# A two-layer hybrid trunk on eight cores: casts of layer 1 into the first FFN phase, residual loads put off, more staging, first loads first

## The chip, the cores and the metric

The kernel runs on the 8 cores of one Trainium2 chip, one batch element per core, with no exchange between the cores. The time is the device time of the slowest core in microseconds (us).

Executions come in two states. In the fast one all cores show a mean granted TensorE clock of 0.973 to 0.989 of full speed. In the slow one the four cores of a die, sometimes of both dies, show a lower one: in one run cores 0 to 3 had a clock of 0.893 to 0.895, while cores 4 to 7 had 0.988. Only fast runs, or the cores of the undisturbed die, are compared here.

## The reference, cut to what matters

```python
D_MODEL, BATCH, SEQ, DEPTH = 1024, 8, 8192, 2
def reference(x, ...):
    h = x
    for l in range(DEPTH):
        mix = token_mixer(h, ...)     # q, k, v, gates; sliding window + forgetting attention; projections
        h = layer_norm(DEEPNORM_ALPHA * h + mix, ...)      # residual 1
        ffn = conv_gated_ffn(h, ...)  # D_FF 2816, 3 causal taps, silu gate
        h = layer_norm(DEEPNORM_ALPHA * h + ffn, ...)      # residual 2
    return h
```

All inputs are float32. The kernel multiplies in bf16, so every weight is cast once on its way.

## The kernel before

The kernel works in four phases: mixer 0, FFN 0, mixer 1, FFN 1, each over 16 tiles of 512 tokens. PE is TensorE, DVE VectorE, ACT ScalarE, POOL GpSimd, SP SyncE. Two engines issue DMAs. POOL issues those that cast float32 to bf16; SP issues the rest, all in one program order:

```python
def cast_some(n=1):                    # POOL: weights float32 in HBM -> bf16 copy in HBM
    for _ in range(n):
        if casts:                      # 30 of layer 0 (w_f1, w_f2), then 76 of layer 1
            key, dst, src = casts.pop()
            i = len(casts) % 8
            POOL.wait(cast_last[i])
            cast_tok[key] = cast_last[i] = POOL.dma(dst, src, so(f"wcast{i}"))
...
# main loop of the mixer: t is the time that the program's builder reckons for PE
if l == 0 and dn.step > 3 and POOL.t <= t and t >= cast_t:
    cast_some()
    cast_t = t + 20e3                  # one every 20 us, all of them in mixer 0
```

The residual of the next tile is loaded into `hf`, the same buffer from which the norm's result has just been stored. The load is therefore behind a wait for that store:

```python
# Norm.apply: the second half of the tile leaves for H1T, then on_done follows at once
SP.wait(t_o)
hf_free[0] = SP.dma(self.hdst_v[:, m - 3:m + 1, ts(self.T)], hf[:, m - 3:m + 1, :], so("hout"))
if m == KC - 1:
    ...
    self.on_done(hf_free[0])           # load_hf(T + 1)
...
def load_hf(self, T):
    SP.wait(hf_free[0], src_tok(self.hsrc, T))      # all later SP work waits here too
    hf_tok[0] = SP.dma(hf, self.hsrc_v[:, :, ts(T)], so("hin"))
```

Q and K go through a ring of staging buffers to HBM, and the attention loads them back in chunks, with V (`kch`, `vch`):

```python
self.st = Ring([E(f"st{i}", [TT], BF16) for i in range(4)])
...
si, sbuf, sfree = st.get()
DVE.wait(sfree)                        # the store of four evictions ago must have landed
t_ev = DVE.sig(nc.vector.tensor_scalar(out=sbuf, in0=bank, ...))
SP.wait(t_ev)
SP.dma(dst[2 * c, 0:64, tsl], sbuf[0:64, :], ...)
```

At the start the constants come first: six loads on SP, memsets, a wait of all engines for them, 32 small stores on SP; after that wait, from POOL, the first activations (`hbp`) and eight weight chunks (`wring`). In layer 0 each chunk is loaded with a cast by POOL and its bf16 copy is stored to `WMD` by SP. Before its first eviction DVE waits for a bias (`bvt`) and a mask.

The softmax here doesn't subtract the row's maximum and nothing guards it: scores larger than these inputs give would overflow.

## Time and profile before

| | us |
|---|---|
| fast runs, same rounds as the changed kernel | 10881, 10885 |
| profiled execution, slowest core (5) | 10831.6 |
| median core of that execution | 10786 |
| slow runs, left out | 11102, 11518 |

Five marks cut the span: the 4th and the 16th load of `hbg` (the gate's activations, one per tile) in each mixer, and the first one of mixer 1. Median over the eight cores of the profiled execution:

| stretch | before, us |
|---|---|
| start to 4th hbg load | 625 |
| mixer 0, 4th to 16th hbg load | 2649 |
| to the first hbg load of mixer 1 (FFN 0 lies here) | 2228 |
| mixer 1, first to 4th hbg load | 542 |
| mixer 1, 4th to 16th hbg load | 2474 |
| rest (FFN 1 lies here) | 2248 |

Mixer 0 and mixer 1 do the same work from the 4th to the 16th load. The prediction reads core 5, on which they are 2700 and 2484 us.

### The profile page before, as it was taken

The page shows a single profiled execution, that of the slowest core. Times are in us where ns is not written, and L with a number is a line of the kernel's source. Part 1 is how long each engine was busy: PE and PEld are TensorE (multiplying, and loading weights), DVE is VectorE, ACT ScalarE, POOL GpSimd, SP SyncE. Part 2 cuts the span into 40 slices and gives each one's busy share as a digit, 9 for nine tenths or more (in the row PEclk, how much of TensorE's full clock was granted, in tenths as well). Part 3 has the DMA queues.
Part 4 walks back from the last instruction along what each step waited for, and adds up shares of the span by engine and source line. Part 5 has one row for each costly group of instructions (what it writes and reads, how often), then busy time and mean ns, then how long its engine had stood idle before and what let it go on. Part 6 is the DMA issues. An engine that isn't in the chain of part 4 may idle for free.

```text
span 10831.6 us, 223078 instructions; the slowest of 8 cores (10746.5 to 10831.6 us)
## 1 busy us (share of the span) xinstructions
PE 10016.4 (92%) x77548; PEld 5139.1 (47%) x77548; DVE 4816.6 (44%) x7633; ACT 6399.9 (59%) x12159; POOL 2722.5 (25%) x2510
## 2 busy tenths in 40 slices
PE   5998898998788999999989999999999889999998
PEld 2444454555455444444434455555555544444443
DVE  3544333332211465566555544333332226566655
ACT  2466787898788332333224678889999863233322
POOL 0212112111111344444431221111110214444444
PEclk8999999999899999999989999999999999999999
DMA  6766766666644311111136665555554441111111
GB/s 136 186 164 169 167 154 160 155 156 149 136 127 113 119 51 44 40 47 47 43 101 157 165 162 152 145 159 148 143 146 128 133 132 51 43 40 50 48 40 43
DMA packets 707722, 1231.95 MB, mean 114 GB/s; under 512 B 64016, under 2 KB 277392, under 8 KB 704400
## 3 DMA queue, kind: packets, MB, share of 16 engines
q1 hardware_dynamic: 595920, 1055.02, 33.3%
q0 software_dynamic: 110720, 162.64, 11.0%
q8 instruction: 662, 10.85, 0.4%
q14 instruction: 420, 3.44, 0.1%
HBM read 1181.07 MB, written 246.69 MB: 132 GB/s over the span
## 4 chain that ended last, share of the span: by engine, by line
PE 66%; POOL 7%; DVE 7%; ACT 7%; DMA 7%; issue 5%; SPq 1%; another core or an unknown queue 1%; DVEq 0%; POOLq 0%; ACTq 0%
PE pD L536 15%; PE pA L877 9%; PE pO L916 7%; PE pB L536 6%; PE pB L877 5%; POOL hf L374 3%; PE pA L1224 3%; PE pO L1224 3%; PE pD L1224 3%; PE pB L1224 3%; ACT pr_134 L886 2%; ACT pr_240 L886 2%; POOL hf L376 2%; SPq L101 1%; PE pA L1186 1%
## 5 line engine op out<-in xcount | busy, mean ns | idle before, releaser
L886 ACT ACTIVATE pr_134<-pA 128x512 bf16<-128x512 f32 (+2 forms) x2414 | 1467.6, 638 | 346.6 <-PE pA L877 280.2
L886 ACT ACTIVATE pr_240<-pA 128x512 bf16<-128x512 f32 (+2 forms) x2414 | 1467.2, 638 | 215.5 <-PE pA L877 149.9
L886 ACT ACTIVATE pr_134<-pB 128x512 bf16<-128x512 f32 (+2 forms) x1330 | 885.3, 666 | 164.9 <-PE pB L877 136.5
L886 ACT ACTIVATE pr_240<-pB 128x512 bf16<-128x512 f32 (+2 forms) x1330 | 885.6, 666 | 103.4 <-PE pB L877 76.8
L374 POOL TENSOR_TENSOR hf<-hf,mean 128x512 f32<-128x512 f32 x512 | 716.8, 1400 | 377.9 <-DVE hf L370 360.9
L326 ACT ACTIVATE sq_60<-hf 128x512 f32<-128x512 f32 x256 | 161.4, 630 | 621.6 <-DVE hf L1227 494.9
L326 ACT ACTIVATE sq_61<-hf 128x512 f32<-128x512 f32 x256 | 161.4, 630 | 615.7 <-DVE hf L1227 525.2
L336 POOL TENSOR_TENSOR acc_q<-acc_q,sq_61 128x512 f32<-128x512 f32 x256 | 324.9, 1269 | 684.3 <-ACT sq_61 L326 680.7
L101 POOL DMA_DIRECT2D hbg_163<-xT x16 | 14.6, 915 | 1563.8 <-PE pO L916 960.3
L370 DVE TENSOR_TENSOR hf<-hf,rstd 128x512 f32<-128x512 f32 x512 | 405.3, 807 | 1.0 <-DVE mean L365 0.5
L101 POOL DMA_DIRECT2D hbg_269<-H2T x16 | 14.2, 886 | 1524.4 <-PE pO L916 1332.6
L916 PEld LDWEIGHTS pO<-vch_0_127,pr_134 128*128 128x128 bf16 x4640 | 269.7, 98 | 204.5 <-issue 27.3
L336 POOL TENSOR_TENSOR acc_q<-acc_q,sq_60 128x512 f32<-128x512 f32 x192 | 243.3, 1267 | 486.5 <-ACT sq_60 L326 483.9
L916 PEld LDWEIGHTS pO<-vch_0_129,pr_134 128*128 128x128 bf16 x4640 | 270.8, 99 | 198.9 <-issue 25.7
L916 PEld LDWEIGHTS pO<-vch_1_233,pr_240 128*128 128x128 bf16 x4640 | 267.9, 98 | 193.7 <-issue 14.8
L916 PEld LDWEIGHTS pO<-vch_1_235,pr_240 128*128 128x128 bf16 x4640 | 267.5, 98 | 191.0 <-issue 13.2
L334 DVE TENSOR_TENSOR acc_r<-acc_r,hf 128x512 f32<-128x512 f32 x448 | 318.0, 710 | 49.8 <-DVE hf L1227 3.2
L916 PEld LDWEIGHTS pO<-vch_0_128,pr_134 128*128 128x128 bf16 x4160 | 240.0, 98 | 180.1 <-issue 20.5
L916 PE MATMUL pO<-vch_0_127,pr_134 128*128 128x65 bf16 x4640 | 315.0, 195 | 10.6 <-issue 10.6
L916 PEld LDWEIGHTS pO<-vch_1_234,pr_240 128*128 128x128 bf16 x4160 | 239.6, 98 | 174.9 <-issue 14.6
L916 PE MATMUL pO<-vch_0_129,pr_134 128*128 128x65 bf16 x4640 | 315.8, 195 | 1.1 <-issue 1.1
L916 PE MATMUL pO<-vch_1_233,pr_240 128*128 128x65 bf16 x4640 | 312.8, 194 | 0.0
(1969 smaller groups left out, 24749.5 us busy)
## 6 DMA issues: line engine op xcount, KB each, us to landing
H1T<-hf SPq DMA_DIRECT2D x64, 1024.0 KB, 5.5
hf<-H1T SPq DMA_DIRECT2D x32, 2048.0 KB, 9.2
hf<-xT SPq DMA_DIRECT2D x16, 2048.0 KB, 12.5
H2T<-hf SPq DMA_DIRECT2D x32, 1024.0 KB, 4.4
hf<-H2T SPq DMA_DIRECT2D x16, 2048.0 KB, 11.4
outT<-hf SPq DMA_DIRECT2D x32, 1024.0 KB, 4.0
wring_1_260<-WMD SPq DMA_DIRECT2D x90, 256.0 KB, 3.6
wring_1_261<-WMD SPq DMA_DIRECT2D x90, 256.0 KB, 3.8
```

The source lines that it names most:

```text
L101: self.e.dma_start(out=out, in_=in_, **kw).then_inc(so.sem, 16)
L326: t_q = ACT.sig(nc.scalar.activation(out=sqb, in_=hf[:, m, :], func=AF.Square))
L334: self.r = DVE.sig(nc.vector.tensor_tensor(out=acc_r, in0=acc_r, in1=hf[:, m, :], op=ALU.add))
L336: self.q = POOL.sig(nc.gpsimd.tensor_tensor(out=acc_q, in0=acc_q, in1=sqb, op=ALU.add))
L370: t = DVE.sig(nc.vector.tensor_tensor(out=hf[:, i, :], in0=hf[:, i, :], in1=rstd, op=ALU.mult))
L374: t_p = POOL.sig(nc.gpsimd.tensor_tensor(out=hf[:, m, :], in0=hf[:, m, :], in1=mean_s, op=ALU.add))
L376: t_o = POOL.sig(nc.gpsimd.tensor_scalar(out=hf[:, m, :], in0=hf[:, m, :], scalar1=self.g_t[:, m:m + 1], scalar2=self.b_t[:, m:m + 1], op0 ...
L536: ins = mm(out, lhsT=lhs(i), rhs=rhs(i), start=(i == 0), stop=(i == n - 1))
L877: ins = mm(sbank[:, c0:c0 + w], lhsT=K[:, jl * 128:(jl + 1) * 128], rhs=Q[:, q0:q0 + w], start=fresh, stop=not diag, skip_group_check=diag)
L886: t_p = ACT.sig(nc.scalar.activation(out=pbuf[:, 0:tot], in_=sbank[:, 0:tot], func=AF.Exp, scale=0.125))
L916: ins = mm(obank[:, i * 65:(i + 1) * 65], lhsT=pbuf[:, cc:cc + 128], rhs=V[:, j % CKB, :], start=state["first"], stop=fin, skip_group_chec ...
L1224: ins = mm(bank, lhsT=wo[m][:, f, :], rhs=at[:, f, :], start=(f == 0), stop=(f == FC - 1))
```

## The change

The intent is to take transfers out of the busy first mixer and put them where the DMA engines are less busy (18% in FFN 0), to keep SP from being held, and to start sooner. There are four parts. The four edits together give the changed kernel.

```diff
 # 1 casts
-            if casts:
-                key, dst, src = casts.pop()
+            if l in casts and casts[l]:
+                key, dst, src = casts[l].pop(0)
...
-                    cast_some()
-                    cast_t = t + 20e3
+                    cast_some(0)
+                    cast_t = t + 60e3
... in the FFN, after each f:
                     ln_step()
+                    if f % 4 == 3:
+                        cast_some(l + 1)
 # 2 residual loads put off: mixer, FFN
-  (lambda t_: self.load_hf(T + 1))
+  (lambda t_: lnq.append((lambda: self.load_hf(T + 1), lambda: ready(t_) + 15e3)))
-  (lambda t_, T=T: self.load_hf(T + 1))
+  (lambda t_, T=T: lnq.extend([(lambda: None, None)] * 4 + [(lambda: self.load_hf(T + 1), None)]))
 # 3 staging
-  self.st = Ring([E(f"st{i}", [TT], BF16) for i in range(4)])
+  self.st = Ring([E(f"st{i}", [TT], BF16) for i in range(8)])
   ... (ons, onr move to another region for space)
 # 4 start
     stages[0].prefetch([])
+    constants()          # the block that stood ahead of everything, unchanged inside
...
-            DVE.wait(t_mk, t_bv)
+  (t_bv before its first use in proj, t_mk before its first use in swa)
```

More of the change, by code (lines that the diff above doesn't have):

```diff
@@ L252, in cvs @@
         return cv[l][:, a:a + n]
-    so_c = so("cst")
-    for l in range(DEPTH):
-        SP.dma(cv[l], cvec[l], so_c)
-        SP.dma(bfn[l], b_f[l], so_c)
-        t0 = SP.dma(esk[l], sinks[l].rearrange("(o n) -> o n", o=1).partition_broadcast(128), so_c)
-    so_p = so("cstp")
-    POOL.dma(identb, c_ident, so_p)
-    t1 = POOL.dma(negmb, c_negm, so_p)
-    ACT.wait(t0)
-    for l in range(DEPTH):
-        t_e = ACT.sig(nc.scalar.activation(out=esk[l], in_=esk[l], func=AF.Exp))
-    DVE.wait(t0, t1, t_e)
@@ L266, in build_program @@
-    nc.vector.memset(onesf, 1.0)
-    nc.vector.memset(eps1, EPS)
-    nc.vector.memset(eps4, 4.0 * EPS)
-    for l in range(DEPTH):
-        nc.vector.tensor_scalar(out=bfn[l], in0=bfn[l], scalar1=-1.0, scalar2=None, op0=ALU.mult)
-        nc.vector.tensor_scalar(out=cvs(l, "bg"), in0=cvs(l, "bg"), scalar1=0.5, scalar2=None, op0=ALU.mult)
-    ones8 = hf.rearrange("p a b -> p (a b)")[0:8, 0:768].bitcast(BF16).rearrange("p (a b) -> p a b", a=3)
-    eights = hf.rearrange("p a b -> p (a b)")[0:8, 1024:1792].bitcast(BF16).rearrange("p (a b) -> p a b", a=3)
@@ L274, in build_program @@
-    nc.vector.memset(ones8, 1.0)
-    t_c = DVE.sig(nc.vector.memset(eights, 8.0))
-    for E in ENGS:
-        E.wait(t_c)
-    for T in range(NT):
-        SP.dma(KBT[:, 64:67, ts(T)], ones8, so("cst8"))
-        t_c8 = SP.dma(QBT[:, 67:70, ts(T)], eights, so("cst8"))
     cast_tok = {}
-    casts = []
+    cast_last = [None] * 8
+    casts = {l: [] for l in range(DEPTH)}
     for l in range(DEPTH):
         if l > 0:
-            for c in range(NPROJ):
-                casts.append((("m", l, c), WMD[l, c], w_mix[l, c]))
-            casts.append((("v", l), WVD[l], w_v[l]))
-            for c in range(NPROJ, NCHUNK):
-                casts.append((("m", l, c), WMD[l, c], w_mix[l, c]))
-        for f in range(FC):
-            casts.append((("f1", l, f), WF1[l, f], w_f1[l, f]))
-        for m in range(KC):
-            casts.append((("f2", l, m), WF2[l, m], w_f2[l, m]))
@@ L296, in build_program, with cast_some @@
-    casts.reverse()
-    cast_last = [None] * 8
-    def cast_some(n=1):
+            casts[l] += [(("m", l, c), WMD[l, c], w_mix[l, c]) for c in range(NPROJ)]
+            casts[l] += [(("v", l), WVD[l], w_v[l])]
+            casts[l] += [(("m", l, c), WMD[l, c], w_mix[l, c]) for c in range(NPROJ, NCHUNK)]
+        casts[l] += [(("f1", l, f), WF1[l, f], w_f1[l, f]) for f in range(FC)]
+        casts[l] += [(("f2", l, m), WF2[l, m], w_f2[l, m]) for m in range(KC)]
+    def cast_some(l, n=1):
         for _ in range(n):
-            if casts:
-                key, dst, src = casts.pop()
-                i = len(casts) % 8
+            if l in casts and casts[l]:
+                key, dst, src = casts[l].pop(0)
+                i = len(cast_tok) % 8
@@ L310, in build_program @@
     hf_tok = [None]
-    hf_free = [t_c8]
+    hf_free = [None]
     lnq = []
@@ L385, in apply, with constants @@
                 self.a = t
+    def constants():
+        so_c = so("cst")
+        for l in range(DEPTH):
+            SP.dma(cv[l], cvec[l], so_c)
+            SP.dma(bfn[l], b_f[l], so_c)
+            t0 = SP.dma(esk[l], sinks[l].rearrange("(o n) -> o n", o=1).partition_broadcast(128), so_c)
+        so_p = so("cstp")
+        POOL.dma(identb, c_ident, so_p)
+        t1 = POOL.dma(negmb, c_negm, so_p)
+        ACT.wait(t0)
+        for l in range(DEPTH):
+            t_e = ACT.sig(nc.scalar.activation(out=esk[l], in_=esk[l], func=AF.Exp))
+        DVE.wait(t0, t1, t_e)
+        nc.vector.memset(onesf, 1.0)
+        nc.vector.memset(eps1, EPS)
+        nc.vector.memset(eps4, 4.0 * EPS)
+        for l in range(DEPTH):
+            nc.vector.tensor_scalar(out=bfn[l], in0=bfn[l], scalar1=-1.0, scalar2=None, op0=ALU.mult)
+            nc.vector.tensor_scalar(out=cvs(l, "bg"), in0=cvs(l, "bg"), scalar1=0.5, scalar2=None, op0=ALU.mult)
+        ones8 = hf.rearrange("p a b -> p (a b)")[0:8, 0:768].bitcast(BF16).rearrange("p (a b) -> p a b", a=3)
+        eights = hf.rearrange("p a b -> p (a b)")[0:8, 1024:1792].bitcast(BF16).rearrange("p (a b) -> p a b", a=3)
+        nc.vector.memset(ones8, 1.0)
+        t_c = DVE.sig(nc.vector.memset(eights, 8.0))
+        for E in ENGS:
+            E.wait(t_c)
+        for T in range(NT):
+            SP.dma(KBT[:, 64:67, ts(T)], ones8, so("cst8"))
+            t_c8 = SP.dma(QBT[:, 67:70, ts(T)], eights, so("cst8"))
+        hf_free[0] = t_c8
     def ln_step(n=1):
@@ L408, in __init__ @@
             self.sp = Ring([E(f"sp{i}", [TT], BF16) for i in range(4)])
-            self.ons = Ring([E(f"ons{i}", [4, 2, 64], BF16) for i in range(2)])
-            self.onr = Ring([E(f"onr{i}", [4, 128], BF16) for i in range(2)])
             E = Region(EA + 72 * 1024, EA + 88 * 1024, f"_{l}")
@@ L420, in __init__ @@
             self.sg = Ring([P(f"sg{i}", [TT], F32) for i in range(4)])
+            self.ons = Ring([P(f"ons{i}", [4, 2, 64], BF16) for i in range(2)])
+            self.onr = Ring([P(f"onr{i}", [4, 128], BF16) for i in range(2)])
             self.mk = P("mk", [2, 2, 512], BF16)
@@ L594, in proj @@
                 vi, svb, svfree = svr.get()
-                DVE.wait(svfree)
+                DVE.wait(svfree, t_bv)
                 vat = va[T % 2]
@@ L646, in swa @@
                 PE.wait(DVE.now())
+                DVE.wait(t_mk)
                 oat = oa[T % 3]
@@ L763, in post @@
                 nrm = Norm(db, eps4, cvs(l, "g1"), cvs(l, "b1"), self.hdst, self.hdst_v, T,
-                           (lambda t_: self.load_hf(T + 1)) if T + 1 < NT else (lambda t_: None))
+                           (lambda t_: lnq.append((lambda: self.load_hf(T + 1), lambda: ready(t_) + 15e3))) if T + 1 < NT else (lambda t_: None))
                 for m in range(KC):
@@ L1096, in run @@
             if l == 0:
-                cast_some(1000)
+                cast_some(0, 1000)
             if pre_next is not None:
@@ L1212, in run @@
                 elif pre_next is not None:
+                    cast_some(l + 1, 1000)
                     pre_next(now())
@@ L1216, in run @@
                 nrm = Norm(fb, eps1, cvs(l, "g2"), cvs(l, "b2"), self.hdst, self.hdst_v, T,
-                           (lambda t_, T=T: self.load_hf(T + 1)) if T + 1 < NT else (lambda t_: None))
+                           (lambda t_, T=T: lnq.extend([(lambda: None, None)] * 4 + [(lambda: self.load_hf(T + 1), None)])) if T + 1 < NT else (lambda t_: None))
                 for m in range(KC):
```

## The prediction

> **What bounds the kernel now.** Of the three timed runs of the kernel before, only the fastest, 10884.82 us, is near the profiled execution (10831.6 us on its slowest core, all cores within 0.8% of each other). The other two, 11102 and 11518 us, are the slow state and are left out, so I work from 10833 to 10885 us.
>
> I read the page's slices first. TensorE (PE) is busy 92% of the span, so the question is where the other 8% lies. The two FFN phases (third and fourth lines' right-hand clock digits all 9, DMA share 1) have almost no idle; the two mixers do, and the first mixer more than the second.
>
> ```profile
> PE   5998898998788999999989999999999889999998
> PEclk8999999999899999999989999999999999999999
> DMA  6766766666644311111136665555554441111111
> ```
>
> The two layers do the same work, so layer 1 is a control for layer 0. I took marks that both have (the loads of hbg, one per tile of 512 tokens, found in the timeline of POOL) and read the busy time between the same two marks of both layers. First column: the stretch, its length, then busy time and instruction count of PE, PEld, DVE, ACT, POOL, then clock, DMA share, GB/s.
>
> ```profile
> 619.00:3319.00 2700.00, 2414.59 (x24044) 1348.03 (x24045) 896.28 (x1645) 2122.95 (x3780) 409.21 (x416) 0.96 0.65 153
> 3627.00:5540.00 1913.00, 1861.53 (x8519) 834.30 (x8517) 1159.63 (x1509) 596.30 (x1601) 836.91 (x754) 1.00 0.18 51
> 6094.00:8578.00 2484.00, 2384.66 (x24031) 1336.09 (x24028) 892.76 (x1644) 2116.99 (x3779) 357.17 (x310) 0.99 0.56 147
> ```
>
> The same 24,000 matmuls took 2700 us in layer 0 and 2484 us in layer 1: 216 us more, of which 30 us are busy time at a lower granted clock (0.96 against 0.99) and 186 us are idle (285 against 99). What only layer 0 has there is the weight casts: 106 DMAs issued from POOL between 641 and 3175 us. The waits of PE and then of the SP queue in the layer 0 stretch show how they hurt:
>
> ```profile
> PE pA L877 <- DMA vch_0_129<-VBD: 50.8, 1, 50.8
> PE pD L607 <- DVE st_0_138 L573: 34.7, 3, 13.6
> PE pA L877 <- DMA vch_0_128<-VBD: 17.5, 1, 17.5
> PE pA L877 <- DMA vch_0_127<-VBD: 16.5, 1, 16.5
> ...
> SPq L86 <- DMA H1T<-hf: 192.6, 12, 57.2
> ```
>
> In layer 1 that last line reads 56.7 us, longest 7.0. SP issues K, V, weight and residual loads in one order; the residual load for the next tile (hf) must wait until the store of H1T has landed, and everything behind it waits too. In the worst case the store took 57 us beside a burst of eight casts that POOL let go at once after it had been held:
>
> ```profile
> 2828.31 3.94 POOL L101 DMA_DIRECT2D WF<-w_f  x8
> ```
>
> The start is the other piece. PE has its first weights at 36.3 us, does three groups, and then stands until 79.8 us:
>
> ```profile
> PE pD L536 <- DMA wring_0_154<-w_mix: 36.3, 1, 36.3
> ...
> PE pD L536 <- DVE qa_141 L566: 36.6, 1, 36.6
> ```
>
> The chain of waits through this window gives 23.36 us of that to the bias load bvt, which SP issued only at 55.39 us, behind 32 small constant stores and eight weight stores; DVE waited for it before its first eviction.
>
> **What the Trainium skill says.** The page "DMA: Bandwidth & Descriptors", section "Issuing engines are not separate DMA queues", says that DMAs of every issuing engine run on the same 16 DMA engines and interleave. The trace agrees: the casts are POOL's, yet SP's store of H1T took 57 us beside them, and a weight chunk landed in 4.0 to 4.5 us in layer 0 against 3.4 to 3.8 in layer 1. The same page, "SWDGE vs HWDGE vs iDMA", says a cast during DMA can only be issued from GpSimd, so the casts cannot leave POOL; only their time can change. "TensorE: Matmul & The Clock Gate", section "What's actually happening", says that the array falls to half clock after an idle window of about 3.4 us; this trace shows a granted clock of 0.50 in the 20 us stretches inside the 50.8 us stall and 0.83 just after it. A removed long stall is thus worth slightly more than its length.
>
> **The change part by part.** The order of instructions, with buffer numbers left out, is identical on PE, DVE and ACT. Only POOL (where casts stand) and SP (where 8 stores and the residual loads stand) differ, plus buffers and waits. So compute cost is unchanged and all of the effect is in waiting.
>
> 1. Casts. Layer 0's mixer keeps 30 of the 106 (22 w_f1 and 8 w_f2), placed singly or in twos, at most three, between POOL's other loads. 216 us over 106 casts is 2.04 us per cast, bursts included; 30 at that rate would cost 61 us. Alone, a cast moves about half or two thirds as much as an hbp load, and layer 1 has those without visible stalls, so I take about half the rate: 30 us. Gain 186 us, in which the 192.6 us of SP blocked on H1T is already contained.
>
> 2. The other 76 go to FFN 0, one per four f steps, five per tile, so all are out in the 16th tile. DMA is only 18% busy there. A cast issue takes POOL 0.5 us. In a tile's first ten f steps POOL is full: per step of 3.45 us it has a conv tap (1.2), two norm operations (1.26 and 1.01) and gaps. PE already loses 51 us over this phase to DVE line 1200, in 49 waits of 1 us, in just these steps. Two of the five casts fall there: 2 x 0.5 us x 16 = 16 us lost; the others fall in steps with 2.7 us of POOL idle and are free. The hb load comes behind a cast but has the second product, 8 x 4.75 = 38 us, to land (9.6 us alone). Cost 15 us.
>
> 3. Start. The first loads go out at about 2 us instead of 12.45, and without the 32 small stores beside them. Before, it took from 12.45 to 36.3 us to have the first weights. But the constants now stand behind eight stores on SP that each wait for a weight chunk, so they come at some 30 us, and PE's first group waits for them. I estimate PE's start at 40 to 50 us, and a wait at the ninth chunk, which POOL can issue only after its memsets. bvt is no longer in the way of the first eviction. The group that began at 79.8 us should begin around 50 and some of it is lost again: gain 25 us.
>
> 4. Staging of eight, residual loads 15 us later: in layer 1, without casts, PE waits some 20 us for staging buffers (8.5, 5.5, 3.3, 3.2) and a vch load (7.1). Most of it goes: 18 us there, and 10 in layer 0 beyond part 1. In the FFN the later residual load (at f = 13 or so of 22) leaves 30 us and the product for a load of 8 to 9 us: nothing either way.
>
> Sum: 186 - 15 + 25 + 28 = 224 us. From 10833 to 10885 this gives 10609 to 10661; I say **10640 us**, a ratio of 0.980 to the fast runs.
>
> **The rivals.** (a) The stall moves instead of going: SP stays held by the waits for POOL's norm before each H1T store (79 us in layer 0, 84 in layer 1) and for PE releases, and 30 casts of the larger kind still meet the K and V loads. For it: the casts kept are the big ones, 1.5 and 2.1 MB of traffic each against 0.75 for a w_mix chunk, so by bytes 36% stay though only 28% by count. Against it: layer 1 has the same SP waits and only 99 us idle. It would leave 80 us of the 216, a time near 10700. (b) POOL becomes the bound of FFN 0: every cast displaces a conv tap, and DVE and PE follow: 76 casts at 1 us, 60 us more than I count, also near 10700. Against it: 837 us of 1913 busy. (c) The casts were most of the trouble and the staging much of the rest, so layer 0 comes out equal to layer 1 and both mixers lose further waits: 216 + 35 + 40 - 10 = 281, near 10580. (d) The start does not shorten, as the constants on SP arrive later than I think: 25 us off, 10665.
>
> **Range and chances.** The gain lies between about 130 us, (a) and (b) partly together, and 320 us. On fast runs that is 10515 to 10755. Two of three runs before were slow by 2 and 6%, so a median with slow runs in it could lie higher; I set 10520 to 10860. The expected gain is almost exactly 2%, so the verdict is nearly even: faster 0.53, same 0.46, slower 0.01.
>
> **What would show each step.** Part 1: in the stretch between the same hbg marks of layer 0, span about 2510 to 2530 us (2700 before), PE idle near 120 us, SP's wait for H1T from 193 to below 40 us. Part 2: FFN 0 within 20 us of its 1913, waits on line 1200 up from 51 to about 65. Part 3: the fourth group of PE near 50 us, the wait on qa gone. Part 4: waits on st below 10 us in all. I am wrong if layer 0's stretch stays above 2600 us (then the casts were not the cause), if FFN 0 grows by over 40 us, or if the start is no earlier.

## More of the kernel before

Where such an undisturbed part is used, the cores and their clock are named.

The median of each stretch is taken by itself, so the column does not sum to the median span.

## The result

The changed kernel's fast runs took 10587.38 and 10605.22 us, and those of the kernel before in the same rounds 10881.27 and 10884.82 us. The ratio of the two means is **0.9737**, 95% interval 0.9695 to 0.9778. The medians of all runs, 10998 us after and 10994 us before, say nothing: each kernel had two slow runs of four.

The same stretches of the changed kernel, medians over eight cores of its profiled execution (fast, 10539 to 10604 us by core):

| stretch | before | after | difference |
|---|---|---|---|
| start to 4th hbg load | 625 | 624 | -1 |
| mixer 0, 4th to 16th | 2649 | 2470 | **-179** |
| FFN 0 | 2228 | 2237 | +9 |
| mixer 1, first to 4th | 542 | 540 | -2 |
| mixer 1, 4th to 16th | 2474 | 2447 | **-28** |
| rest, FFN 1 | 2248 | 2249 | +1 |
| span of the median core | 10786 | 10571 | -215 |

Medians of stretches do not add up. The means over the eight cores do: 193 us less in mixer 0, 31 less in mixer 1 (29 of them from the 4th to the 16th load), 8 more in FFN 0, and nothing at the start or in FFN 1, in all 215 us.

The page of the changed kernel, slices of the span in tenths:

```profile
PE   5899999999988999999979999999999889999998
PEclk8999999999999999999989999999999999999999
DMA  6867666666444222233356666655554441111111
```

DMA now has 2 and 3 where FFN 0 lies (1 before), and 6, then 4 in the second half of mixer 0. The first digit of PE is 5 as before. The stretches of the slowest core, here core 4, with the columns as in the prediction:

```profile
625.00:3098.00 2473.00, 2347.05 (x23582) 1335.44 (x24038) 896.03 (x1644) 2118.29 (x3779) 373.43 (x340) 0.99 0.62 154
...
5881.00:8350.00 2469.00, 2348.95 (x23587) 1335.25 (x24042) 895.70 (x1645) 2119.18 (x3780) 357.72 (x311) 0.99 0.57 148
```

On this core the mixers now take the same time, 2473 and 2469 us, at the same clock (0.96 and 0.99 before); by the medians 23 us are left between them. The PE column must not be compared with that of before: this trace has 23582 matmul records where the weight loads number 24038, so some 2% are missing. The waits tell it without that fault. PE's longest waits in the mixer 0 stretch:

```profile
PE pA L874 <- ACT pr_74 L883: 32.8, 45, 4.1
PE pB L874 <- ACT pr_74 L883: 12.9, 16, 2.6
PE pD L532 <- ACT sg_0_110 L733: 11.3, 9, 1.5
```

Stalls on V loads (50.8, 17.5, 16.5 us) and on the staging evictions stood here before. Now the first lines are the softmax on ACT, in waits of 0.7 to 0.8 us on average and at most 4.1 (line 883, 886 before). All of PE's waits in the stretch sum to 98 us, against 279 on core 5 before; the rows that wait on a V load sum to 0.6 us against 93.1, and those on staging are gone (56.0). On all eight cores the sum is now 69 to 98 us, against 226 to 284. SP's list began with the same three lines before, and its fourth was the wait for the store of H1T, 192.6 us; this one has no row any more:

```profile
SPq L86 <- PE pD L532: 648.2, 256, 8.3
SPq L86 <- PE pO L913: 405.1, 168, 13.0
SPq L86 <- PE pB L532: 278.7, 112, 11.2
SPq L86 <- POOL hf L343: 83.6, 22, 5.9
```

The start, PE's waits in the first 130 us:

```profile
PE pD L532 <- DVE va_0_89 L518: 56.2, 1, 56.2
PE pB L532 <- DMA wring_0_94<-w_mix: 13.5, 1, 13.5
```

PE starts at 56.2 us instead of 36.3. It is then not stopped at the fourth group, but at the ninth. The chain of waits of the first 100 us says what held it (start, duration, what):

```profile
6.34 33.74 DMA wring_0_101<-w_mix
42.68 7.12 DMA esk_51<-attn_sinks
56.21 5.39 PE pD L532 x16
65.70 19.48 DMA wring_0_94<-w_mix
```

The eighth weight chunk landed at 40 us; only then did SP, which had to store it, issue the constants. They landed at 49.8 us, and ACT's and DVE's work on them lasted until PE could start. POOL had waited for the same constants until 55.9 us, then did 8.4 us of memsets; so the ninth chunk was issued only at 65.70 us, right behind the 1 MB load of hbg, and took 19.48 us. The ninth group began at 85.4 us, against 90.4 before.

### The profile page after: what moved, and what is told of

The parts are those of the page before. It is cut to its first block, busy times and chain, and to the rows that moved or that the text cites. A ratio compares the mean times of both kernels' runs of the same rounds, so it can differ in the third digit from the quotient of the medians.

```text
span 10603.7 us, 221590 instructions; the slowest of 8 cores (10539.2 to 10603.7 us)
## 1 busy us (share of the span) xinstructions
PE 9864.4 (93%) x76060; PEld 5124.7 (48%) x77548; DVE 4822.7 (45%) x7633; ACT 6398.0 (60%) x12159; POOL 2717.5 (26%) x2510
## 4 chain that ended last, share of the span: by engine, by line
PE 71%; ACT 8%; DVE 7%; POOL 6%; issue 5%; DMA 3%; DVEq 0%; SPq 0%; POOLq 0%; ACTq 0%; another core or an unknown queue 0%
PE pD L532 17%; PE pA L874 9%; PE pO L913 9%; PE pB L532 7%; PE pB L874 5%; PE pA L1224 3%; PE pD L1224 3%; PE pO L1224 3%; PE pB L1224 3%; ACT pr_74 L883 3%; ACT pr_184 L883 3%; POOL hf L341 2%; PE pA L1183 1%; PE pO L1183 1%; PE pD L1183 1%
```

## The experiments

Medians over all eight cores of a fast profile, unless a die is named:

| run | start to 4th hbg | mixer 0 | FFN 0 | mixer 1, late | span |
|---|---|---|---|---|---|
| before | 625 | 2649 | 2228 | 2474 | 10786 |
| casts alone | 628 | 2531 | 2235 | 2482 | 10670 |
| put-off alone | 627 | 2567 | 2228 | 2447 | 10670 |
| start alone | 627 | 2649 | 2231 | 2477 | 10791 |
| changed kernel | 624 | 2470 | 2237 | 2447 | 10571 |
| before, cores 4 to 7 | 621 | 2677 | 2230 | 2480 | 10802 |
| staging alone, cores 4 to 7 | 624 | 2628 | 2228 | 2454 | 10723 |
| changed kernel, cores 4 to 7 | 624 | 2473 | 2237 | 2455 | 10583 |
| changed, staging of four, cores 4 to 7 | 633 | 2465 | 2234 | 2448 | 10566 |
| changed, without put-off, cores 4 to 7 | 628 | 2493 | 2235 | 2453 | 10596 |
| changed, casts at 20 us, cores 4 to 7 | 631 | 2503 | 2231 | 2448 | 10602 |
| changed kernel, cores 0 to 3 | 624 | 2461 | 2237 | 2446 | 10556 |
| changed, casts in bursts in FFN 0, cores 0 to 3 | 622 | 2468 | 2231 | 2449 | 10562 |

**Theory.** The casts fill the DMA engines in bursts, the store of H1T takes long beside them, and SP, held by its wait for that store, issues K, V and weight loads late. **Rival.** The order of loads on SP is the cause, and the casts are only one more load.

### Casts alone

The edit is part 1 of the diff above, on the kernel before.

> The kernel before with only the weight casts changed: layer 1's 76 casts in FFN 0, the 30 of layer 0 at 60 us. Stretch medians over the eight cores before: layer 0 between the fourth and last hbg load 2649 us, FFN 0 stretch 2228, layer 1 mixer 2474. Theory (the casts are the cause of layer 0's excess over layer 1): layer 0's stretch falls by 120 to 170 us, to 2480 to 2530, FFN 0 grows by about 9, layer 1 stays at 2474 within 10, and the time falls by 1.2 to 1.7%. Rival (the order of loads on SP is the cause, the casts only one more load): layer 0 falls by less than 60 us, the time by less than 0.5%.

Mixer 0 fell by 118 us, at the low edge of what the theory said, FFN 0 grew by 7, and the two fast runs, 10702.52 and 10736.0 us, are 1.3% under the one fast run of the kernel before on this chip, 10860.5. The rival's "less than 60" falls. But 61 us of the 179 are not there, and the waits on the slowest core (2) show what is left; PE, then SP (lines between left out):

```profile
PE pA L872 <- DMA vch<-VBD: 15.1, 2, 13.2
PE pB L531 <- DVE st L568: 11.8, 2, 8.7
...
SPq L86 <- DMA H1T<-hf: 87.0, 12, 13.7
```

SP still waits 12 times for H1T, 87 us instead of 193 (83 to 95 by core, 169 to 196 before), the longest 13.7 us instead of 57.2. So the prediction's part 1, which counted this wait as gone with the casts, does not hold for almost half of it.

### Put-off alone

The edit is part 2 alone, so all 106 casts stay in mixer 0.

> The kernel before with only the residual loads (hf) put off. Theory of the casts: the put-off takes SP's wait for the store of H1T out of the way (193 us in layer 0 to below 40), so the one long stall of 50 us and parts of others go even with all 106 casts in place: layer 0's stretch 2649 to about 2570 to 2610, layer 1's 2474 to about 2460. Rival (order of loads is the main cause): layer 0 falls by 120 us or more, near 2520, and layer 1 by all of its 28. Time 0.5 to 0.9% down in the first case, over 1.2% in the second.

Mixer 0 fell by 82 us, just beyond the theory's 39 to 79 and short of the rival's 120. Mixer 1 fell by 28, all that the whole change gains there, as the rival had it. The one fast run, 10696.25 us, is 1.5% under 10860.5, which is also more than the theory's 0.9. So both causes are real. What stays of PE's waits, on core 0, are loads that are late beside the casts:

```profile
PE pA L877 <- DMA vch<-VBD: 47.5, 4, 31.5
PE pA L877 <- ACT pr L886: 32.4, 43, 4.1
PE pD L536 <- DMA wring<-WMD: 18.9, 2, 10.5
PE pB L536 <- DMA wring<-WMD: 14.4, 1, 14.4
```

The wait for H1T has left SP's list. The waits on the staging evictions fell from 56.0 us to 0.7 in mixer 0 and from 17.2 to none in mixer 1, with four buffers still: they had come from stores that stood behind SP's wait. In the sum, casts and put-off alone give 118 + 82 = 200 us, together with the rest 179: they share some 20 us (28 by the means over the cores).

### Staging alone

The edit is part 3 alone. It was run twice.

> The kernel before with only eight staging buffers for Q and K instead of four. Theory: the waits on st in layer 0 (56 us of PE waiting directly on its evictions on the profiled core) go to below 15, but a part of that time comes back as waits for K and V loads as the SP order is unchanged: layer 0's stretch falls by 15 to 45 us, layer 1's by 8 to 20. Rival (staging hides nothing that other waits would not): both within 8 us.

Both dies were throttled in the profile of this run (clock 0.89 and 0.93), so its medians over the cores say nothing. But cores 0, 1, 6 and 7 had 0.97 in mixer 0 (0.96 before) and took 2590 to 2628 us there, and cores 2 to 5 had 0.99 or more in mixer 1 and took 2449 to 2457. Its one fast time, 10756.44 us, is 1.0% under 10860.5.

> The kernel before with eight staging buffers again, for a profile in the fast state (the first one fell in the slow state and its stretches cannot be compared). Put-off alone took PE's waits on the staging evictions from 56.0 to 0.7 us in layer 0 and from 17.2 to none in layer 1 with four buffers. Theory (both parts cure the same wait): staging alone also takes these waits below 15 us; layer 0's stretch 2649 falls by 15 to 45 us and layer 1's 2474 by 8 to 20. Rival (independent gains): layer 0 falls by 45 us or more, which with 118 for the casts and 82 for the put-off would exceed the 179 of the whole by far.

Here cores 4 to 7 were undisturbed (clock 0.98). Against the same cores of the kernel before, mixer 0 fell by 49 us and mixer 1 by 26. That is more than the theory's 15 to 45 and 8 to 20, and the 49 passes the rival's mark of 45; but the four cores before differ among themselves by 62 us in mixer 0. Over the ten undisturbed passes of a core through mixer 0 in both profiles (also cores 2 and 3 here) the median is 2616 us, 33 under the 2649 of all cores before, inside the theory's range; over the ten through mixer 1 it is 2452, 22 under. Whether the gains are independent is settled by the runs without one part, below. The waits on staging are gone, as expected. SP is still held as long, and the wait has partly moved, PE and then SP on core 5:

```profile
PE pA L877 <- DMA vch<-VBD: 98.7, 9, 40.2
...
PE pB L877 <- DMA vch<-VBD: 15.3, 2, 11.3
...
SPq L86 <- DMA H1T<-hf: 186.6, 12, 45.9
```

PE's waits on V loads are 114 us, against 93.1 before on the same core (114 to 144 against 76 to 102 over cores 4 to 7). The bigger ring lets the stores be late; it does nothing for the loads that are late for the same reason.

### The changed kernel without one part

With `range(8)` of the staging ring back at `range(4)`:

> The changed kernel with four staging buffers instead of eight. Theory: the put-off has already removed the wait that the buffers bridge: layer 0's stretch stays at 2470 within 10 us, layer 1's at 2447 within 5, PE's waits on staging below 5 us. Rival: layer 0 grows by 20 us or more.

Mixer 0 is at 2465 us and mixer 1 at 2448, no slower than with eight buffers (2473 and 2455 on the same cores), and no wait on staging is left. In the changed kernel the doubled staging is worth nothing: the put-off has removed what it bridges.

With `on_done` calling `load_hf(T + 1)` at once again, in mixer and FFN:

> The changed kernel with the residual loads as before. Theory: eight buffers bridge part of SP's waits for the store of H1T, and with few casts these are short (87 us in all in the run with casts alone): layer 0's stretch 2470 grows to 2480 to 2510, layer 1's 2447 to 2452 to 2470. Rival (the put-off is needed as such, since SP also holds K, V and weight loads): layer 0 above 2515, layer 1 back at 2474.

Mixer 0 grew by 20 us, as expected; mixer 1 did not (2453 against 2455), where the theory had 5 us or more. With few casts and eight buffers there is not much left for the put-off. On core 5 SP's wait for H1T is back at 85.9 us and PE's waits on V loads at 37.6:

```profile
PE pA L874 <- DMA vch<-VBD: 25.5, 4, 14.9
PE pB L874 <- DMA vch<-VBD: 12.1, 3, 5.4
...
SPq L86 <- DMA H1T<-hf: 85.9, 12, 13.8
```

### Casts of layer 0 at 20 us

```diff
-                    cast_t = t + 60e3
+                    cast_t = t + 20e3
```

> The changed kernel with layer 0's 30 casts at 20 us instead of 60: bursts of four and five instead of one and two, over about four tiles instead of twelve. Theory (with the residual loads put off and 76 casts gone, a burst stops only the transfers beside it): layer 0's stretch 2470 grows by 5 to 30 us. Rival (spacing is the main part of the cast change): it grows by 50 us or more. Second rival (spacing is worth nothing): within 5 us.

Mixer 0 grew by 30 us (2503 against 2473), at the top of the theory's range. The same 30 casts then stand over four tiles, more than half of them in runs of four and five right behind POOL's hbp loads, and PE's waits on weight chunks are 24.9 us on core 5 (13 to 42 on cores 4 to 7, at most 7 on any core of the changed kernel):

```profile
PE pD L532 <- DMA wring<-WMD: 24.9, 4, 8.5
```

With the put-off in place, the whole cast change is worth about 97 us in mixer 0 (2567 with the put-off alone, 2470 changed; the doubled staging adds nothing). Some 30 of them come from spacing the 30 casts, and the larger part, about 67, from moving the other 76.

### Casts of FFN 0 in bursts

```diff
-                    if f % 4 == 3:
-                        cast_some(l + 1)
+                    if f == 20:
+                        cast_some(l + 1, 5)
```

> The changed kernel with the five casts of each FFN 0 tile issued at once at f = 20, ahead of the next hb load, instead of one every four f. Theory (the transfers have slack there: DMA 18% busy before, and hb has 38 us of the second product to land): hb lands later than its 10.5 us, 25 to 35 us, and the FFN 0 stretch, 2237, changes by less than 8 us; it may even lose the few us that the casts cost in the norm's steps. Rival (the spread is needed): hb comes later than the product ends, and the stretch grows by 40 us or more.

The stretch fell by 6 us, so spreading the casts in the FFN is not needed and even costs a little. A finer pair of marks, the second and the last load of hb in FFN 0 (14 tiles), has 1671.4 us before, 1675.5 in the changed kernel and 1671.3 with bursts (medians over the cores named above), with spreads under 5 us among cores. I was wrong on hb's landing: 11.8 to 14.8 us by core instead of 25 to 35. A cast of 512 KB lands in 9.7 us here (core 1), against 5.7 in the changed kernel (core 4) and 30.2 before, inside mixer 0 (core 5).

### The start

Alone, on the kernel before (part 4):

> The kernel before with only the first loads issued first, and the waits for the bias and the mask moved to their use. The changed kernel gained nothing up to the fourth hbg load (625 us before, 624 after, medians of eight cores). Theory: the first group of PE starts near 56 us instead of 36, is not stopped at the fourth, but waits 10 to 15 us at the ninth weight chunk, which stands behind the hbg load on POOL: the fourth hbg load at 615 to 635 us, all other stretches as before within 15 us. Rival: the part gains 15 to 25 us by itself, hidden in the changed kernel by another part; then the fourth hbg load is at 600 to 610.

The 4th hbg load came at 627 us, and all other stretches were as before. PE's waits had the form of the changed kernel's, with a wait on one of the four staging buffers after them (slowest core, 0):

```profile
PE pD L538 <- DVE va L524: 57.4, 1, 57.4
PE pB L538 <- DMA wring<-w_mix: 16.7, 1, 16.7
PE pD L538 <- DVE st L575: 13.3, 1, 13.3
```

The part is worth nothing as it is. The single time, 10814 us against 10860.5, shows how little one run tells: its median span is 5 us above that of the kernel before.

To test why, the start was mended: SP loads the constants before anything else, the eight weight stores are emitted later, PE waits for the identity only before its first transpose, and the first hbg and hf loads go out after the first projection.

```diff
     def constants():
+        stages[0].late = []            # w_pump puts its WMD stores here
         (six loads on SP)
+        stages[0].prefetch([])
...
-        DVE.wait(t0, t1, t_e)
+        hf_ident[0] = t1               # PE waits for it in swa
+        DVE.wait(t0, t_e)
... (KBT, QBT constants on SP)
+        for x in stages[0].late:
+            x()
...
-            self.load_hbg(0, tok0)
-            lnq.append((lambda: self.load_hf(0), lambda: 0.0))
             for _ in proj(0):
                 ln_step()
+            self.load_hbg(0, tok0)
+            lnq.append((lambda: self.load_hf(0), lambda: 0.0))
```

> The changed kernel with its start mended: SP loads the constants at once, the eight weight stores come after them, PE waits for the identity at its first transpose only, and the first hbg and hf loads go out after the first projection. Theory (the change's start failed because the constants stood behind the stores, and the ninth weight chunk behind the hbg load): PE starts at 25 to 30 us instead of 56, the ninth group by 55 us instead of 85, and the fourth hbg load comes at 585 to 605 us instead of 624; all else within 10 us of the changed kernel, 10535 to 10560 us in fast runs. Rival (DMA bandwidth sets the start, the order of loads does not): the ninth group at 75 us or later, the fourth hbg load above 612.

All nine runs were slow, so its time does not count. In the profile the granted clock from 100 to 600 us was 0.77 on cores 0, 1, 6 and 7, but 0.93 to 0.94 on cores 2 to 5, as in the changed kernel (0.91 to 0.93). On these four the 4th hbg load came at 595 to 606 us, where the theory had 585 to 605, and mixer 0 took 2452 to 2473, as in the changed kernel. PE started at 27.9 to 30.0 us on all cores, also as expected. But the ninth group began at 59 to 66 us, neither the theory's 55 nor the rival's 75: its chunk had to wait for the store of the first one, which stood behind the 32 small stores.

The next version emits the eight stores ahead of those.

> The changed kernel with its start mended once more: as e7, but the eight weight stores go out ahead of the 32 small constant stores, since in e7 the ninth weight chunk could be loaded only when the first chunk's store, behind these, had landed (56 us). In e7 the second hbp load (end of the first projection) came at 91 to 94 us on four cores against 107 to 114 in the changed kernel, before the throttle came on. Theory: PE starts at 25 to 30 us, the ninth group by 55 us, the second hbp load at 80 to 88, and the fourth hbg load at 590 to 608 against 624; all other stretches as in the changed kernel within 10 us, so 0.2% faster in all. Rival (what follows the start is bound by transfers, which the earlier start only meets earlier): second hbp load early, but fourth hbg load within 8 us of 624.

The profile was fast: on its slowest core (3) PE started at 29.9 us and the ninth group began at 57.9, 3 us later than expected. The 4th hbg load came at 591 to 611 us, median 602 against 624. PE's waits on that core:

```profile
PE pD L546 <- DMA wring<-w_mix: 29.9, 1, 29.9
PE pB L546 <- DMA wring<-w_mix: 11.6, 1, 11.6
PE pA L888 <- DMA vch<-VBD: 10.9, 1, 10.9
```

Order was what held the start back; how much each of the moved pieces is worth alone was not run. Moving hbg also makes the hbg marks of mixer 1 shift, so FFN 0 and the early part of mixer 1 are taken together: 2286 + 478 = 2764 us against 2237 + 540 = 2777. That 13 us I had not expected. It is not in FFN 0, whose 14 tiles take 1675.1 us as in the changed kernel (1675.5), and the four cores 2 to 5 of the version before have it too (2762 to 2770); its cause was not looked for. The span of the median core is 10525 us (10571), the single fast run 10551.26.

### The best version

The mended start with the bursts in FFN 0:

> The best version so far: the mended start of e10 with the burst of e8. e10's medians over eight cores: fourth hbg load 602 us (624 in the changed kernel), span 10525 (10571); e8 on its undisturbed die had the FFN 0 stretch at 2231 against 2237. Theory (the two gains are in different stretches and add up): span median 10515 to 10530, fast runs 10530 to 10560 us, 0.4% under the changed kernel and 2.8 to 3.1% under the kernel before. Rival: the burst's gain is noise between cores and the span stays at 10525 or above; the difference is then not worth a claim.

Three fast runs: 10546.06, 10551.84 and 10559.57 us, mean 10552, which is 0.4% below the changed kernel's mean of 10596 and about 3.0% below the 10883 of the kernel before. These are runs of different rounds; in its own rounds the kernel before had no run near its fast times (one of 11168.92 us is labelled fast, but all its cores read a clock of 0.939 to 0.944, so it is left out). FFN 0 and the early part of mixer 1 take 2282 + 478 = 2760 us, 4 less than without the burst. The span of the median core is 10535 us, not under e10's 10525, since mixer 0 came out 9 us longer. So the mended start is shown to help. The burst helps FFN 0 itself: its 14 tiles take 1671.4 to 1671.7 us on all eight cores, against 1675.1 to 1675.5 without it. That these 4 us show in the whole is not shown.

## Why the prediction was right, and where it was not

**Part 1, casts (186 us expected).** The place and size held: the mixer 0 stretch fell by 179 us over the median of the cores, for which parts 1 and 4 together had 196. The reading of layer 1 as the control held too: after the change mixer 0 is 23 us above mixer 1, near the 30 us left for 30 casts. Two things were off. The excess was taken from core 5, the slowest, with 216 us; the median core's was 2649 - 2474 = 175 and the mean 178, so the page of the slowest core overstates it (core 4 has 2700 us as well, the other six 2631 to 2655). And the gain was booked to the casts, with SP's wait for H1T "already contained"; this was the wrong step of part 1. Casts alone gave 118 us and left 87 us of that wait. The other 61 came with the put-off, which gives 82 when alone: with it and four buffers everything is there (2465), and without it the eight buffers bring all but 20 us (2493 against 2473, cores 4 to 7). Part 4, which holds these two, had been given 10 us in this mixer.

**Part 2, FFN 0 (15 us expected).** The stretch grew by 9 us, and by 4.1 over 14 tiles between the finer marks: 0.3 us per tile, where the step had two casts at 0.5 us in full. The waits on the gate's evictions (line 1200, now 1197) went from 51.0 to 53.2 us, medians of the cores, where the step had 65; with bursts they are back at 51.1. So the mechanism, casts in the norm's steps, fits at about a quarter of its size, and these waits carry about half of the 4.1 us; the rest of the 9 us was not traced. Rival (b), 60 us more, falls.

**Part 3, start (25 us expected).** This step failed: the gain was 1 us, and the rival (d) came true. The step had the constants at 30 us and PE's start at 40 to 50; they were issued at 40.5 us, behind the eighth chunk, landed at 49.8, and PE began at 56.2, after work on ACT and DVE that the step had not counted. It named the wait at the ninth chunk without a size; it was 13.5 us. The step had POOL's memsets ahead of that chunk, but not POOL's own wait for the constants nor the hbg load. The mended versions change both orders at once and bring the start forward; they show that order was the cause, and not how it divides.

**Part 4, staging and put-off (18 us in mixer 1, 10 in mixer 0).** Mixer 1 gained 28 us, so the sum's term was too small there. (Of the four waits that it gives for staging, the one of 3.3 us is on another eviction, `rcr`; staging had 17.2 on that core.) The step did not see that the two parts cure one wait: each gives all of it alone (28 and 26 us), and after one the other is worth nothing in mixer 1.

**Rivals (a) and (c).** (a) had 80 us of mixer 0's excess stay; 23 did. (c), both mixers losing further waits, was nearest in mixer 1.

**The sum.** 224 us expected, 215 by the spans of the median cores and 287 by the timed fast runs (10883 - 10596). The timed fast runs of before, 10881 and 10885, lie some 50 us above its profiled execution of 10833, so the profiled pair gives 228; fast runs of that kernel in later rounds took 10859 to 10865. The time of 10640 was 44 us above the fast runs' mean. That the sum came so near is in part luck. By the means over the cores mixer 0 gave 193 us where parts 1 and 4 had 196, mixer 1 gave 31 where the sum had 18, FFN 0 cost 8 instead of 15, and the start gave nothing instead of 25: the missing 25 us were made up by 13 and 7 elsewhere. The even chances for 2% were too cautious: the interval, 2.2 to 3.1% faster, lies wholly beyond it. They rested on the ratio of 0.980, which is 10640 over the middle of the two bases, 10859; over the timed fast run of 10885 it is 0.9775.

## What to carry to other kernels

When two phases do the same work, use the quieter one as control and compare marks over all cores, not the slowest core's page alone. Where one engine issues all loads in order, a load that must wait for a store's landing should be issued when that store has surely landed; more buffers only hide part of such a wait. Putting the first loads first helps only if what the first instruction needs, constants included, is not queued behind their completion.

## What the Trainium skill lacked or had wrong

- "DMA: Bandwidth & Descriptors", section "Anatomy of one DMA — SWDGE (gpsimd) path": its fit, 2.0 us plus bytes over 436e3 per us, makes 4.4 us for 1 MB. In FFN 0 before, with a DMA share of 0.18, a load that casts 2 MB of float32 to 1 MB of bf16 landed in 9.6 us (median of 16); counting the 2 MB read the fit makes 6.8. A figure for loads that cast is lacking.
- The same page, section "Issuing engines are not separate DMA queues": it says that transfers interleave and that the choice of the issuing engine saves only sequencer time. The section has no number for what one transfer suffers from the others (a cast of 512 KB landed in 30.2 us in mixer 0 before and in 5.7 us in FFN 0 of the changed kernel; the longest wait for a 1 MB store was 57.2 us). Nor does it draw out the case that decided here: a wait on the issuing engine holds all loads behind it. Taking that wait away in each tile (193 us of SP in mixer 0) was by itself worth 82 us.
- "TensorE: Matmul & The Clock Gate", section "Seeing it yourself": it says that a third core of a die with dense matmuls takes the whole die to 13/16 of the clock while the load lasts, and to budget this for all cores. The slow run with the mended start shows the value, 0.81 at 400 to 600 us on core 0. But in every fast run all eight cores had mean clocks of 0.973 to 0.989, with PE busy 92% and 93% of the span in the two kernels' pages, and in the slow profiles two cores of a die had the low clock while the other two had the fast one in the same part of their spans. Each core's times count from its own start, so which parts ran at the same moment cannot be read from these traces, and when which clock holds stays open.
